# A decoder layer on one Trainium2 core: gates of two dense blocks written by accumulating scatters instead of one-hot products

## The chip, the cores and the metric

The kernel runs on one core of a Trainium2 chip. The metric is the time of one execution on the device in microseconds (us), as the median of several runs. The trace comes from a further execution, taken by the hardware profiler.

## What is computed

The program is one decoder layer for 512 tokens of width 1024: sparse attention and a state space mixer side by side, cross-attention to a memory, and an expert mixer. The change lies in the expert mixer (`peer_ffn`), which has 128 x 128 = 16384 experts of one neuron each. A token picks 16 experts in each of 8 heads, and its 128 gates go to softmax, head by head:

```python
s_top, i_top = lax.top_k(s, PEER_TOPK)                  # s: tokens x 8 heads x 2 sides x 128 keys
cand = (s_top[:, :, 0, :, None] + s_top[:, :, 1, None, :]).reshape(n, PEER_HEADS, PEER_TOPK * PEER_TOPK)
sc, ci = lax.top_k(cand, PEER_TOPK)
e_a = jnp.take_along_axis(i_top[:, :, 0], ci // PEER_TOPK, axis=-1)
e_b = jnp.take_along_axis(i_top[:, :, 1], ci % PEER_TOPK, axis=-1)
experts = e_a * PEER_N_KEYS + e_b
gw = jax.nn.softmax(sc, axis=-1)
act = jax.nn.gelu(jnp.einsum('td,tkd->tk', xb, u_tab[experts]))
out = jnp.einsum('tk,tkd->td', gw * act, v_tab[experts])
```

## The kernel before

The 512 tokens are four blocks of 128. Block 3 takes the experts' rows one by one: 256 gathers (128 rows of `utab`, `gather_u`, line 857; 128 of `vtab`, `gather_v`, line 870), each an indirect transfer of 128 rows of 4 KB that GpSimd issues, followed by a VectorE instruction over the landed tile (lines 859 and 874). The tiles `gr` come from a pool of seven buffers.

Blocks 0 to 2 (384 tokens) are dense: for each of the 128 values `a` of the first key, all 128 experts of that value are worked on for all 384 tokens. `layer1(a)` (line 840) loads 128 rows of u (512 KB), splits them in two parts (ScalarE makes `uh`, VectorE makes `ul`, lines 88 and 89), and multiplies them with the activations in 24 matmuls. `layer2(a)` (line 1072) multiplies that with a tile of gates (`mf`, line 1081), splits it and the rows of v, and `sum_up` adds 18 matmuls to the sums `yo` (line 1095). The gates are dense there too: a matrix of expert by token that is zero but for 128 values in each token's column. It lies in device memory as the tensor `wd`, and `load_w` (line 1098) brings in the gates of eight values of `a` at a time.

The stages in order of time:

- **Choosing** (lines 897 to 995). `project(h)` makes the scores of a head on TensorE; `head(h)` finds the best 16 on VectorE (lines 927 to 949); `decode(h)` turns positions into expert numbers (lines 952 to 983): `slA` and `slB` hold the two key numbers of each choice, `gidx` the expert number for block 3, `slW` the scores. `decode` of a head runs in the course of the next one. To keep TensorE busy, `keep_some` calls `layer1` for 76 values of `a` ahead of time and stores the results in device memory ("kept" products, `gd`); some gathers for block 3 are issued too (`P1G`).
- **Softmax** of all heads at once (lines 997 to 1004).
- **Gates** (lines 1034 to 1064). For each dense block, `turned` transposes `slA`, `slB` and `slW`; then, for each group of 16 tokens, VectorE builds four one-hot tiles (`oa`, `ob`, `obh`, `obl`, lines 1050 to 1053), TensorE multiplies them in 32 matmuls of 128 x 128 (`ps_w`, lines 1058 and 1059), ScalarE moves the result to `stg` in four instructions (line 1060), and a store of 1 MB writes it to `wd` (line 1062). Beside each of the 24 groups one or two more products are kept.
- **Summing** (lines 1134 to 1179): `layer2` and `sum_up` for all 128 values of `a`, `layer1` for the 52 that were not kept, and the rest of the gathers between them.

Within each engine instructions run in the order that a scheduler gave them when the program was built. SyncE issues the loads in such an order too; ScalarE issues the stores, GpSimd the gathers. Where one instruction needs another one's data, or its buffer, it waits for a semaphore, and all behind it on the same engine waits too.

Of the kernel before, what the change touches and what calls it, by code (L numbers as in the profile page):

```python
# [9 lines left out]
F32 = mybir.dt.float32  # L10
# [31 lines left out]
for _n, _w in (("ident", 128), ("tri", 128), ("cneg", 128), ("iota", 128),  # L42
               ("inv", 2)):
    CC[_n] = _at
    _at += _w
# [10 lines left out]
A8 = 8  # L56
P1G, P2G = 2, 0
NEARLY = 2
DELAY = 3
# [3 lines left out]
def tile_hybrid(ctx, tc, xT, memT, pos, prm, cst, win, wab, wsb, wou, wcq, wckv, wco, wpq, subk, uT, utab, vtab,  # L63
# [117 lines left out]
    atx = ExitStack()  # L181
    at = atx.enter_context(tc.tile_pool(name="at", bufs=1))
    wkA = ExitStack()
    wk = wkA.enter_context(tc.tile_pool(name="wk", bufs=2))
# [220 lines left out]
    def conv(j, dst):  # L405
# [15 lines left out]
        if j > 3:  # L421
            choose_some(3)

    zd = dram.tile([16, 128, T], F32, name="zd")
    gad = dram.tile([16, 128, T], F32, name="gad")

    def spill(ch, dst, func):
        ps = proj(ch)
        t = gen("spill")
        S.activation(t, ps, func, scale=0.5 if func == AF.Tanh else 1.0)  # L430
        S.dma_start(dst, t)

    for g in range(4):
        for j in range(4):
            conv(4 * g + j, xchunk(4 * g + j))
            spill(CH_Z + 4 * g + j, zd[4 * g + j], AF.Silu)
            if 4 * g + j:
                next(stepper, None)
        conv(16 + g, bT[g])
        conv(20 + g, cT[g])  # L440
# [342 lines left out]
    gp = ctx.enter_context(tc.tile_pool(name="gp", bufs=7, reuse_waits="tile"))  # L783
    wd = dram.tile([DENSE // TG, 128, 128 * TG], F32, name="wd")
    gd = dram.tile([N_KEPT, 128, DENSE], F32, name="gd")
# [134 lines left out]
    def head(h, sS, before):  # L920
# [22 lines left out]
        for b in order:  # L943
# [5 lines left out]
            V.max_index(ci[:, b, 8:16], slW[:, b, h * 16 + 8:h * 16 + 16], c_)  # L949
        return ci, ti  # L950

    def decode(h, ci, ti):

# [27 lines left out]
        for p, sl_ in ((0, slA), (1, slB)):  # L981
            V.tensor_tensor(sl_[:, :, hs], oh[:, 4 * p:4 * p + 4, 0], oh[:, 4 * p:4 * p + 4, 1], op=OP.add)
        V.scalar_tensor_tensor(gidx[:, hs], slA[:, 3, hs], 128.0, slB[:, 3, hs], op0=OP.mult, op1=OP.add)

    chosen = None
    sS = project(0)
    choosing[0] = True
    for h in range(9):
# [6 lines left out]
        chosen = nxt_chosen  # L995

    sw = slW.rearrange("p b (h s) -> p (b h) s", s=16)
    top = sp.tile([128, 32], F32, name="top", bufs=1)
    V.tensor_copy(top, sw[:, :, 0])
    V.tensor_tensor(sw, sw, top[:, :, None].to_broadcast([128, 32, 16]), op=OP.subtract)  # L1000
    S.activation(slW, slW, AF.Exp)
    V.tensor_reduce(top, sw, axis=AX.X, op=OP.add)
    V.reciprocal(top, top)
    V.tensor_tensor(sw, sw, top[:, :, None].to_broadcast([128, 32, 16]), op=OP.mult)
    V.tensor_copy(gwt, slW[:, 3, :])
# [27 lines left out]

    nxt = turned(0)
    for b in range(NTB):
        eT = nxt
        for g in range(128 // TG):
# [16 lines left out]
            for q in range(TG // 4):  # L1054
                ps = psum("sm", "ps_w")
                for i in range(4):
# [4 lines left out]
                             ps.rearrange("b (t a) -> b t a", t=4), AF.Copy, scale=1.0 / 32768)  # L1061
            S.dma_start(wd[b * (128 // TG) + g], stg.rearrange("b a t -> b (a t)"))
            keep_some(2 if b * 8 + g < NEARLY else 1)
            gather_some(P2G)
    keep_some(N_KEPT)
    se2.close()
# [31 lines left out]
    def load_w(j):  # L1098
        W8 = mp.tile([128, DENSE // TG, A8 * TG], F32, name="W8", tag="W8")
        SY.dma_start(W8, bass.AP(tensor=wd.tensor, offset=wd.offset + j * A8 * TG,  # L1100
                                 ap=[[128 * TG, 128], [128 * 128 * TG, DENSE // TG], [1, A8 * TG]]))
        return W8
# [79 lines left out]
def _constants():  # L1182
# [5 lines left out]
    for d, j in ((128, 0), (64, 1)):  # L1188
        half = d // 8
        inv = np.float32(500000.0) ** (np.float32(-2.0) * np.arange(half, dtype=np.float32) / np.float32(2 * half))  # L1190
        for base in range(0, 128, d):
            c[base:base + half, CC["inv"] + j] = inv
            c[base + 32:base + 32 + half, CC["inv"] + j] = -inv
    c[:, CC["iota"]:CC["iota"] + 128] = i[None, :]
    return c

# [76 lines left out]
```

## Time and profile before

| | |
|---|---|
| median of 3 runs | 2185.63 us (2183.03 to 2190.58) |
| the profiled execution | 2189.17 us, its span 2187.4 us |
| mean granted TensorE clock | 0.984 of full speed |
| busy in the span | TensorE 97%, VectorE 72%, ScalarE 45%, GpSimd 33% |
| moved by DMA | 469.26 MB, mean 215 GB/s |

The span runs from the first to the last instruction; the remaining 1.8 us of the execution lie around it. In the rows further down, PE is TensorE's matmuls, PEld its weight loads, DVE VectorE, ACT ScalarE, POOL GpSimd, and SPq the DMA queue of SyncE. A busy share is an average over stages with different limits, so the stages are read one by one.

### The profile page before, as it was taken

The page shows a single profiled execution, that of the slowest core. Times are in us where ns is not written, and L with a number is a line of the kernel's source. Part 1 is how long each engine was busy: PE and PEld are TensorE (multiplying, and loading weights), DVE is VectorE, ACT ScalarE, POOL GpSimd, SP SyncE. Part 2 cuts the span into 40 slices and gives each one's busy share as a digit, 9 for nine tenths or more (in the row PEclk, how much of TensorE's full clock was granted, in tenths as well). Part 3 has the DMA queues.
Part 4 walks back from the last instruction along what each step waited for, and adds up shares of the span by engine and source line. Part 5 has one row for each costly group of instructions (what it writes and reads, how often), then busy time and mean ns, then how long its engine had stood idle before and what let it go on. Part 6 is the DMA issues. An engine that isn't in the chain of part 4 may idle for free.

```text
span 2187.4 us, 29926 instructions
## 1 busy us (share of the span) xinstructions
PE 2111.0 (97%) x11039; PEld 1817.2 (83%) x11039; DVE 1575.6 (72%) x2954; ACT 977.2 (45%) x1513; POOL 718.7 (33%) x412
## 2 busy tenths in 40 slices
PE   8999999999999999999998999999999999999997
PEld 6888778877788777798988899988888888888886
DVE  8576744489952434499999588578778888788885
ACT  4444355665642334343434377643333333333333
POOL 2444432344324433204332000024344444444430
PEclk8999999999999999999999999999999999999999
DMA  4333322376453422248776477899999999999982
GB/s 136 110 109 115 105 90 85 106 213 179 144 177 98 130 78 82 101 138 315 262 244 223 133 259 260 287 324 367 333 327 336 339 352 327 341 330 327 345 287 70
DMA packets 209137, 469.26 MB, mean 215 GB/s; under 512 B 16064, under 2 KB 109376, under 8 KB 205792
## 3 DMA queue, kind: packets, MB, share of 16 engines
q1 hardware_dynamic: 153120, 284.63, 40.6%
q0 software_dynamic: 36864, 134.23, 16.7%
q10 hardware_dynamic: 19008, 48.51, 5.8%
q8 instruction: 86, 1.41, 0.3%
q14 instruction: 59, 0.48, 0.1%
HBM read 416.64 MB, written 50.66 MB: 214 GB/s over the span
## 4 chain that ended last, share of the span: by engine, by line
PE 78%; DVE 14%; ACT 3%; DMA 2%; issue 2%; POOL 1%; SPq 0%; DVEq 0%; ACTq 0%
PE yo L1095 24%; PE ps_u L138 18%; PE ps_in L138 15%; PE pss L138 4%; DVE ul L89 2%; PE ps_cq L138 2%; PE ps_h L138 2%; DVE gr L859 2%; PE ps_o L138 2%; PE ps_q L138 1%; PE ps_kv L138 1%; PE ps_w L1058 1%; PE ps_w L1059 1%; PE ps_l L459 1%; PE po L494 1%
## 5 line engine op out<-in xcount | busy, mean ns | idle before, releaser
L89 POOL TENSOR_TENSOR wl<-wr,wh 128x1024 fp32r<-128x1024 f32 x122 | 300.7, 2465 | 527.0 <-PE ps_in L138 166.7
L857 POOL DMA_INDIRECT gr<-utab,gidx x128 | 187.1, 1461 | 580.0 <-DVE gr L859 462.4
L138 PE MATMUL ps_u<-fH,uh 128*128 128x384 f32 x1024 | 349.5, 341 | 11.7 <-ACT uh L88 11.7
L138 PE MATMUL ps_u<-fL,uh 128*128 128x384 f32 x1024 | 345.7, 338 | 0.0
L870 POOL DMA_INDIRECT gr<-vtab,gidx x128 | 187.8, 1467 | 242.4 <-DVE acc L874 218.5
L88 ACT CAST vh<-vr 128x1024 fp32r<-128x1024 f32 x128 | 134.4, 1051 | 225.4 <-PE yo L1095 170.6
L138 PE MATMUL ps_in<-aH,wh 128*128 128x512 f32 x536 | 215.3, 402 | 4.0 <-ACT wh L88 2.8
L88 ACT CAST wh<-wr 128x1024 fp32r<-128x1024 f32 x135 | 141.3, 1047 | 167.9 <-PE ps_in L138 83.3
L138 PE MATMUL ps_in<-aL,wh 128*128 128x512 f32 x536 | 211.3, 395 | 0.3 <-DVE aL L89 0.3
L138 PE MATMUL ps_u<-fH,ul 128*128 128x384 f32 x1024 | 202.0, 338 | 9.7 <-DVE ul L89 9.3
L138 PEld LDWEIGHTS ps_u<-fH,uh 128*128 128x128 f32 x1024 | 194.2, 190 | 14.9 <-ACT uh L88 12.7
L1095 PE MATMUL yo<-vh,mh 128*128 128x512 f32 x768 | 199.0, 394 | 3.5 <-ACT mh L1085 3.5
L89 DVE TENSOR_TENSOR vl<-vr,vh 128x1024 fp32r<-128x1024 f32 x128 | 156.3, 1223 | 58.5 <-ACT vh L88 48.8
L1095 PE MATMUL yo<-vh,ml 128*128 128x512 f32 x768 | 198.4, 393 | 0.0
L1095 PE MATMUL yo<-vl,mh 128*128 128x512 f32 x768 | 197.5, 392 | 0.0
L138 PEld LDWEIGHTS ps_u<-fL,uh 128*128 128x128 f32 x1024 | 194.6, 190 | 1.9
L138 PEld LDWEIGHTS ps_u<-fH,ul 128*128 128x128 f32 x1024 | 180.6, 190 | 14.6 <-DVE ul L89 14.6
L89 DVE TENSOR_TENSOR ul<-ur,uh 128x1024 fp32r<-128x1024 f32 x82 | 103.6, 1265 | 120.5 <-ACT uh L88 65.0
L1095 PEld LDWEIGHTS yo<-vh,ml 128*128 128x128 f32 x768 | 145.1, 189 | 31.9
L1095 PEld LDWEIGHTS yo<-vl,mh 128*128 128x128 f32 x768 | 144.6, 188 | 31.7
L1095 PEld LDWEIGHTS yo<-vh,mh 128*128 128x128 f32 x768 | 144.2, 189 | 31.8 <-ACT mh L1085 3.8
L874 DVE SCALAR_TENSOR_TENSOR acc<-gr,gwt,acc 128x1024 f32<-128x1024 f32 x127 | 163.1, 1284 | 0.8
(450 smaller groups left out, 4032.2 us busy)
## 6 DMA issues: line engine op xcount, KB each, us to landing
vr<-vtab SPq DMA_DIRECT2D x128, 512.0 KB
ur<-uT SPq DMA_DIRECT2D x80, 512.0 KB
wr<-win SPq DMA_DIRECT2D x71, 512.0 KB
cr<-uT SPq DMA_DIRECT2D x48, 512.0 KB
wd<-stg ACTq DMA_DIRECT2D x24, 1024.0 KB
W<-wd SPq DMA_DIRECT2D x16, 1536.0 KB
gd<-ga ACTq DMA_DIRECT2D x76, 192.0 KB
gk<-gd SPq DMA_DIRECT2D x76, 192.0 KB
```

The source lines that it names most:

```text
L88: S.copy(hi, src)
L89: return (lo_eng or V).tensor_tensor(lo, src, hi.bitcast(F32), op=OP.subtract)
L138: TE.matmul(ps[:m, :n], w_[:, k, :m], x_[:, k, :n], start=first and i == 0, stop=last and i == len(order) - 1)
L459: TE.matmul(ps[:, :n], qT[:, b * 128:(b + 1) * 128], kT[h // 4][:, :n], start=True, stop=True)
L494: TE.matmul(po[:, b * 128:(b + 1) * 128], vt[:, s, (h // 4) * 128:(h // 4 + 1) * 128], pt[:, s * 128:(s + 1) * 128], start=s == 0, stop=s ...
L857: G.indirect_dma_start(out=r[:], out_offset=None, in_=utab[:, :], in_offset=bass.IndirectOffsetOnAxis(ap=gidx[:, k:k + 1], axis=0))
L859: return lambda: V.scalar_tensor_tensor(r, r, 1.0, afg, op0=OP.mult, op1=OP.mult, accum_out=gdot[:, k:k + 1])
L870: G.indirect_dma_start(out=r[:], out_offset=None, in_=vtab[:, :], in_offset=bass.IndirectOffsetOnAxis(ap=gidx[:, k:k + 1], axis=0))
L874: return lambda: V.scalar_tensor_tensor(acc, r, gwt[:, k:k + 1], acc, op0=OP.mult, op1=OP.add)
L1058: TE.matmul(w_ps, obh[at_], oa[at_], start=True, stop=False)
L1059: TE.matmul(w_ps, obl[at_], oa[at_], start=False, stop=True)
L1095: TE.matmul(yo[b][i], m[:, b * 128:(b + 1) * 128], v[:, i * 512:(i + 1) * 512], start=a == seq[0] and p == 0, stop=a == seq[-1] and p == 2)
```

## The change

The gates of blocks 0 and 1 are no longer made by one-hot products. `wd` becomes three tensors, one for each dense block. Those of blocks 0 and 1 are filled with zeros early in the program (`clear_gates`, 16 stores of 1 MB from SyncE). The softmax is done head by head: `head` makes the exponentials, `decode` the sums and the gates. `decode` then computes where each gate belongs (`wx`, from `slA`, `slB` and a new constant column `place`) and issues 16 indirect transfers for each of the two blocks. Each of them adds 128 single numbers, one for each token, to places in device memory. That is 32 in a head and 256 in all, 128 on each tensor. Block 2 keeps its eight groups of one-hot products. `P1G` goes from 2 to 0 (no gathers in the code of the heads); beside each group two products are kept, and the last twelve kept products have three gathers each beside them (`P3G`).

```diff
-P1G, P2G = 2, 0
-NEARLY = 2
+NSC = 2
+P1G, P3G = 0, 3
...
+    zeros = at.tile([128, 128], F32, name="zeros")
+    G.memset(zeros, 0.0)
...
+    wd = [dram.tile([128 * 128 * 128, 1], F32, name=f"wd{b}") for b in range(NTB)]
+    wdg = [w.rearrange("(g b f) o -> g b (f o)", b=128, f=128 * TG) for w in wd]
+
+    def clear_gates(i):
+        if i < NSC * (128 // TG):
+            w = wdg[i // (128 // TG)][i % (128 // TG)]
+            SY.dma_start(w.rearrange("b (r f) -> b r f", f=128), zeros[:, None, :].to_broadcast([128, TG, 128]))
...
             spill(CH_Z + 4 * g + j, zd[4 * g + j], AF.Silu)
+            clear_gates(4 * g + j)
...
-        return ci, ti
-
-    def decode(h, ci, ti):
+        ex = sp.tile([128, 4, 16], F32, name="ex", tag="ex")
+        hw = slW[:, :, h * 16:(h + 1) * 16]
+        V.tensor_tensor(ex, hw, hw[:, :, 0:1].to_broadcast([128, 4, 16]), op=OP.subtract)
+        S.activation(ex, ex, AF.Exp)
+        return ci, ti, ex
+
+    def decode(h, ci, ti, ex):
...
+        sm = sp.tile([128, 4], F32, name="sm", tag="sm")
+        V.tensor_reduce(sm, ex, axis=AX.X, op=OP.add)
+        V.reciprocal(sm, sm)
+        V.tensor_tensor(slW[:, :, hs], ex, sm[:, :, None].to_broadcast([128, 4, 16]), op=OP.mult)
+        wi = sp.tile([128, NSC, 16], F32, name="wi", tag="wi")
+        V.tensor_scalar(wi, slA[:, :NSC, hs], float(TG), cs[:, CC["place"]:CC["place"] + 1], op0=OP.mult, op1=OP.add)
+        wx = sq.tile([128, NSC, 16], I32, name="wx", tag="wx")
+        V.scalar_tensor_tensor(wx, slB[:, :NSC, hs], float(128 * TG), wi, op0=OP.mult, op1=OP.add)
+        for s in range(16):
+            for b in range(NSC):
+                G.indirect_dma_start(out=wd[b][:, :], out_offset=bass.IndirectOffsetOnAxis(ap=wx[:, b, s:s + 1], axis=0),
+                                     in_=slW[:, b, h * 16 + s:h * 16 + s + 1], in_offset=None, compute_op=OP.add)
...
-    nxt = turned(0)
-    for b in range(NTB):
+    nxt = turned(NSC)
+    for b in range(NSC, NTB):
...
-            S.dma_start(wd[b * (128 // TG) + g], stg.rearrange("b a t -> b (a t)"))
-            keep_some(2 if b * 8 + g < NEARLY else 1)
-            gather_some(P2G)
-    keep_some(N_KEPT)
+            S.dma_start(wdg[b][g], stg.rearrange("b a t -> b (a t)"))
+            keep_some(2)
+    while kept[0] < N_KEPT:
+        keep_some(1)
+        gather_some(P3G)
...
-        SY.dma_start(W8, bass.AP(tensor=wd.tensor, offset=wd.offset + j * A8 * TG,
-                                 ap=[[128 * TG, 128], [128 * 128 * TG, DENSE // TG], [1, A8 * TG]]))
+        for b in range(NTB):
+            SY.dma_start(W8[:, b * (128 // TG):(b + 1) * (128 // TG), :],
+                         wdg[b][:, :, j * A8 * TG:(j + 1) * A8 * TG].rearrange("g b f -> b g f"))
```

The scheduler orders the changed program anew. Three places matter. In these rows a number behind a name tells buffers apart, and the brackets name the semaphores that a row waits for: `DMASW` with a number counts the ends of GpSimd's transfers, which take the numbers 0 to 7 in turn; `DMAHW` those of other transfers; the rest are engines. The first is GpSimd's queue from the first expert numbers on. Before:

```order
L89 TENSOR_TENSOR fL<-ft,fH 128x512 x4
L857 DMA gr<-utab,gidx 128x1024 x128
L870 DMA gr<-vtab,gidx 128x1024 x128
L1123 TENSOR_TENSOR htm<-htm,gf 128x1024 x2
L1269 UNCONDITIONAL_BRANCH
```

In the change (`wd0` and `wd1` are the gates of blocks 0 and 1):

```order
L89 TENSOR_TENSOR fL_7320<-ft_7424,fH_7319 128x512 [waits Activation_49]
L868 DMA gr_11795<-utab,gidx_7324 128x1024 [waits DVE_49]
L1009 DMA wd0_493<-slW_7342,wx_8031 2097152x1 [waits DVE_49]
L1009 DMA wd1_494<-slW_7342,wx_8031 2097152x1
L868 DMA gr_11797<-utab,gidx_7324 128x1024 [waits Pool_49]
L1009 DMA wd0_493<-slW_7342,wx_8031 2097152x1 [waits DMASW1_49]
L1009 DMA wd1_494<-slW_7342,wx_8031 2097152x1 [waits DMASW2_49]
L868 DMA gr_11799<-utab,gidx_7324 128x1024 [waits Pool_49]
L1009 DMA wd0_493<-slW_7342,wx_8031 2097152x1 [waits DMASW4_49]
L1009 DMA wd1_494<-slW_7342,wx_8031 2097152x1 [waits DMASW5_49,DMASW0_49]
L868 DMA gr_11835<-utab,gidx_7324 128x1024
```

The 256 scatters stand where gathers stood, in pairs, one for each tensor. With the numbers counted on from 0 at the first gather, the first scatter on `wd0` has 1, and the next one on `wd0` waits for 1: each scatter waits for the end of the one before it on the same tensor. 34 gathers stand between pairs, all of them ahead of the scatters of head 3; the other 222 stand behind the last scatter. The second place is VectorE, where the positions `wx` of head 2 are made. Before, `gidx` follows its two inputs with no wait for a transfer:

```order
L930 MAX tv_8988<-sS_8543 128x8 [waits DVE_49]
L982 TENSOR_TENSOR slA_7320<-oh_8719 128x4x16 [waits DVE_49]
L982 TENSOR_TENSOR slB_7321<-oh_8719 128x4x16
L931 MAX_INDEX ti_8989<-tv_8988,sS_8543 128x8 [waits DVE_49]
L983 SCALAR_TENSOR_TENSOR gidx_7303<-slA_7320,slB_7321 128x16 [waits DVE_49]
L928 MAX_INDEX ti_8989<-tv_8988,sS_8543 128x8
```

In the change:

```order
L997 TENSOR_TENSOR slA_7340<-oh_8786 128x4x16 [waits DVE_49]
L997 TENSOR_TENSOR slB_7341<-oh_8786 128x4x16
L1004 TENSOR_SCALAR wi_8799<-slA_7340,cs_60 128x32 [waits DVE_49]
L998 SCALAR_TENSOR_TENSOR gidx_7324<-slA_7340,slB_7341 128x16 [waits DVE_49]
L942 MAX_INDEX ti_9075<-tv_9074,sS_8610 128x8
L1006 SCALAR_TENSOR_TENSOR wx_8801<-slB_7341,wi_8799 128x32 [waits DMASW4_49,DMASW3_49,DMASW6_49,DMASW1_49,DMASW7_49,DMASW0_49,DVE_49]
L939 MAX_INDEX ti_9075<-tv_9074,sS_8610 128x8 x2
L89 TENSOR_TENSOR ul_8892<-cr_8889,uh_8891 128x1024 [waits DMAHW2_49,PE_49,Activation_49]
```

`wx` has two buffers, so that of head h waits for the scatters of head h - 2, and the split `ul` of a kept product stands behind it. In this order 26 of the 76 kept products have their `ul` behind the `wx` of head 7. The third place is SyncE's queue around the first load of gates, `W8`. Before, all loads of u for kept products stand ahead of it, and one for a fresh product (`ur_12801`):

```order
L827 DMA ur_12754<-uT 128x1024 [waits DMAHW7_49,DMAHW1_49,DVE_49]
L1075 DMA vr_12838<-vtab 128x1024 [waits DMAHW0_49,PE_49]
L1075 DMA vr_12903<-vtab 128x1024 [waits DMAHW2_49]
L1075 DMA vr_12939<-vtab 128x1024 [waits DMAHW3_49]
L827 DMA ur_12801<-uT 128x1024 [waits DMAHW5_49,DMAHW4_49,DVE_49]
L1110 DMA gf_12799<-gfin 128x1024 [waits DMAHW7_49,PE_49]
L1100 DMA W8_12834<-wd_7312 128x24x128 [waits DMAHW4_49,DMAHW6_49,DMAHW1_49,PE_49]
```

In the change:

```order
L838 DMA ur_11841<-uT 128x1024 [waits DMAHW7_49,DMAHW1_49,DVE_49]
L1120 DMA W8_12314<-wd0_493 128x8x128 [waits DMASW4_49,DMASW5_49,DMASW3_49,DMASW6_49,DMASW2_49,DMASW7_49,DMASW1_49,DMAHW5_49,DMASW0_49,PE_49]
L838 DMA ur_11881<-uT 128x1024 [waits DMAHW3_49,DMAHW2_49,DVE_49]
L1120 DMA W8_12314<-wd1_494 128x8x128
L838 DMA ur_11924<-uT 128x1024 [waits DMAHW7_49,DMAHW5_49,DVE_49]
L1120 DMA W8_12314<-wd2_495 128x8x128 [waits DMAHW6_49,DMAHW4_49,DMAHW0_49]
```

The load of gates waits for the last scatters of both tensors, and the loads of u for the last nine kept products and for three further ones stand behind it. All twelve products stand ahead of the first `yo` matmul on TensorE; before, there was one fresh product there, so two of them are work of the summing stage done earlier.

## Rows read from the trace of the kernel before

**Rows 1.** The page: busy us, share and instructions of each engine.

```profile
PE 2111.0 (97%) x11039; PEld 1817.2 (83%) x11039; DVE 1575.6 (72%) x2954; ACT 977.2 (45%) x1513; POOL 718.7 (33%) x412
```

**Rows 2.** Stretches of the span: busy us of each engine, TensorE clock, DMA.

```profile
core 0: us, PE busy (x) PEld busy (x) DVE busy (x) ACT busy (x) POOL busy (x), PEclk, DMA share, GB/s
0.00:928.00 928.00, 894.99 (x4430) 721.12 (x4431) 547.81 (x915) 433.88 (x816) 339.11 (x154) 0.98 0.39 121
928.00:1240.00 312.00, 298.31 (x1613) 279.36 (x1612) 279.63 (x1112) 126.89 (x162) 73.73 (x55) 0.99 0.66 222
1240.00:1420.00 180.00, 168.25 (x1443) 164.07 (x1444) 144.98 (x136) 128.60 (x149) 0.00 (x0) 0.96 0.71 256
1420.00:2187.00 767.00, 749.47 (x3557) 652.63 (x3555) 603.22 (x792) 287.83 (x387) 305.89 (x203) 0.99 0.90 314
```

**Rows 3.** The matmuls and the evictions of the one-hot products, ns min/median/max.

```profile
L1058 PE MATMUL ps_w<-oa,obh x384: 218/218/312, 1244.2 to 1408.0; 128*128 128x128 f16 x192
...
L1060 ACT ACTIVATE stg<-ps_w x96: 1052/1124/1168, 1246.3 to 1409.6; 128x512 f32<-128x512 f32 x96
```

**Rows 4.** TensorE in time, one-hot products: start, length, [idle before <-releaser].

```profile
1244.16 0.61 PE L1058 MATMUL ps_w<-oa,obh 128*128 128x128 f16 x4 [5.40 <-DVE obh L1052]
...
1256.37 0.24 PE L1058 MATMUL ps_w<-oa,obh 128*128 128x128 f16 x1
...
1258.19 0.42 PE L138 MATMUL ps_u<-fH,uh 128*128 128x384 f32 x1
```

**Rows 5.** Groups of instructions, a one-hot tile: busy us, mean ns.

```profile
L1050 DVE TENSOR_TENSOR oa<-io,e 128x2048 f16<-128x2048 f16 x24 | 29.3, 1219 | 0.0
```

**Rows 6.** TensorE in time, kept products one after another.

```profile
1412.35 0.33 PE L138 MATMUL ps_u<-fH,uh 128*128 128x384 f32 x1
...
1416.51 0.33 PE L138 MATMUL ps_u<-fH,uh 128*128 128x384 f32 x1
...
1419.28 1.55 PE L138 MATMUL ps_u<-fH,ul 128*128 128x384 f32 x8
```

**Rows 7.** The expert numbers of eight heads, first and last start.

```profile
L983 DVE SCALAR_TENSOR_TENSOR gidx<-slA,slB x8: 146/154/174, 982.7 to 1204.7; 128x16 int32<-128x16 f32 x8
```

**Rows 8.** GpSimd in time, gathers back to back and one after a wait.

```profile
983.16 1.11 POOL L857 DMA_INDIRECT gr<-utab,gidx  x1 [61.43 <-DVE ti L928]
...
990.19 0.94 POOL L857 DMA_INDIRECT gr<-utab,gidx  x1 [0.30 <-issue]
991.43 0.94 POOL L857 DMA_INDIRECT gr<-utab,gidx  x1 [0.30 <-issue]
992.68 0.94 POOL L857 DMA_INDIRECT gr<-utab,gidx  x1 [0.30 <-issue]
...
1010.25 1.68 POOL L857 DMA_INDIRECT gr<-utab,gidx  x1 [2.35 <-DVE gr L859]
```

**Rows 9.** VectorE in time, the first gathers landing.

```profile
987.85 1.23 DVE L859 SCALAR_TENSOR_TENSOR gr<-gr,afg 128x1024 f32<-128x1024 f32 x1 [0.63 <-DMA gr<-utab,gidx]
...
996.97 1.23 DVE L859 SCALAR_TENSOR_TENSOR gr<-gr,afg 128x1024 f32<-128x1024 f32 x1 [0.48 <-DMA gr<-utab,gidx]
...
1002.91 1.22 DVE L859 SCALAR_TENSOR_TENSOR gr<-gr,afg 128x1024 f32<-128x1024 f32 x1 [0.45 <-DMA gr<-utab,gidx]
```

**Rows 10.** The start in time: a small load, its user, a table load.

```profile
0.75 1.28 ACT L337 ACT_TABLE_LOAD   x1 [0.75 <-PEq L1262]
0.75 0.38 SPq L194 DMA_DIRECT2D pr<-prm  x1
...
2.71 0.20 ACT L337 ACTIVATE na<-pr 32x1 f32<-32x1 f32 x1 [0.68 <-DMA pr<-prm]
```

**Rows 11.** The first load of gates and its user in time.

```profile
1420.22 0.38 SPq L1100 DMA_DIRECT2D W<-wd  x1
...
1429.00 0.56 DVE L1081 TENSOR_TENSOR mf<-gk,W 128x384 f32<-128x384 f32 x1 [2.18 <-DMA gk<-gd]
```

**Rows 12.** TensorE in time, the first matmuls of the sums.

```profile
1430.15 2.07 PE L1095 MATMUL yo<-vh,mh 128*128 128x512 f32 x4 [3.51 <-ACT mh L1085]
```

More of the change, by code (lines that the diff above doesn't have):

```diff
@@ L42 @@
 for _n, _w in (("ident", 128), ("tri", 128), ("cneg", 128), ("iota", 128),
-               ("inv", 2)):
+               ("inv", 2), ("place", 1)):
     CC[_n] = _at
@@ L783, in tile_hybrid @@
     gp = ctx.enter_context(tc.tile_pool(name="gp", bufs=7, reuse_waits="tile"))
-    wd = dram.tile([DENSE // TG, 128, 128 * TG], F32, name="wd")
     gd = dram.tile([N_KEPT, 128, DENSE], F32, name="gd")
@@ L995, in tile_hybrid @@
         chosen = nxt_chosen
[L997 to L1004, printed above, removed]
     V.tensor_copy(gwt, slW[:, 3, :])
@@ L1194, in _constants @@
     c[:, CC["iota"]:CC["iota"] + 128] = i[None, :]
+    c[:, CC["place"]] = i // TG * (128 * 128 * TG) + i % TG
     return c
```

## The prediction, written before the changed kernel ran

> **What bounds the kernel now.** The page's busy times come first: TensorE is busy for 2111 of 2187.4 us [rows 1], so work taken off TensorE shortens the kernel as long as nothing else makes it wait. The table by stretches shows where the change acts [rows 2]. Ahead of 928 us nothing of it runs but the zero fill. From 928 to 1240 (choosing) TensorE is busy for 298 of 312 us and VectorE for 280, so both are nearly full. From 1240 to 1420 (gates and kept products) TensorE is busy for 168 of 180 us and GpSimd does nothing. From 1420 on (summing) TensorE is busy for 749 of 767 us at a DMA share of 0.90. So a microsecond of TensorE in the gates' stage is worth about one, while GpSimd has time to spare on average. What decides is whether GpSimd's new work ends in time, since the sums can't begin without the gates.
>
> **What is taken away.** A group of one-hot products lasts 1.82 us on TensorE once it runs, from 1256.37 to 1258.19 [rows 4]; 16 of the 24 groups go: 16 x 1.82 = 29 us off TensorE's path. The wait of 5.40 us ahead of the first group [rows 4] stays, since block 2 has a first group too. VectorE loses four tiles of 1.22 us in each group [rows 5], 16 x 4 x 1.22 = 78 us, and ScalarE four evictions of 1.12 us [rows 3], 72 us. Neither bounds that stage, so these count nothing. The most that can be won is about 30 us.
>
> **Small additions, counted as nothing.** The zero fill is 16 MB in a stretch whose DMA share is 0.39 and where TensorE is busy for 895 of 928 us [rows 2]; at the 314 GB/s of the summing stage it is 53 us of transfers in 16 portions. Behind a portion a weight load is some 3 us late, which the loads' lead should cover; without that cover it would be up to 53 us. The exponentials by head bring two table loads to each head, 1.28 us each [rows 10], 16 x 1.28 = 20 us on ScalarE, which is busy for 127 of 312 us while heads are chosen. Fourteen more gathers are left for the summing stage (222 against 208), 7 MB or 23 us at its rate, and 18 us of VectorE; a tenth of 767 us of DMA time is free there, so TensorE covers them, and bare they would cost 23 us.
>
> **What is added to a path: the chain of scatters.** Each scatter waits for the end of the one before it on the same tensor, and the two tensors go side by side. So 128 pairs follow each other, and the length of a pair is the larger of two things: GpSimd's time to issue two scatters (three transfers where a gather stands between), or the time from a scatter's start on GpSimd to its last write.
>
> *Issue.* The trace has no scatter; the nearest row is a gather, which also makes 128 rows of descriptors from a list. Back to back they start every 1.24 us (990.19, 991.43, 992.68) [rows 8]. Two make 2.48 us, three 3.72 us. After a real wait one takes 1.68 us where 0.94 is usual [rows 8].
>
> *End of a scatter, from below.* A small plain load, issued at 0.75 us, has its user start at 2.71: 1.96 us [rows 10]. An indirect transfer has GpSimd's part besides; but if an end came within 2.48 us, issue would bound the pair.
>
> *From above.* The first gather starts at 983.16 on GpSimd [rows 8] and its user, which waited for it, at 987.85 [rows 9]: 4.69 us, with 512 KB moved. A scatter moves 512 bytes but reads its places before it writes them, so even this isn't a firm ceiling.
>
> *What I take.* The nearest row is the gather without its payload. The fourth to the seventh gather land in 996.97 to 1002.91 [rows 9], 1.98 us each, so the payload is some 2.0 us and 2.7 us are left. That gather took 1.11 us on GpSimd; after a wait, as every scatter, it is 1.68, which adds 0.6. For the reading before the writing I add another 0.6, an estimate between nothing and a second trip of 1.96 us. So a pair takes 3.9 us, with a gather between 3.9 + 1.24 = 5.1 us. 34 pairs have a gather, 94 have none: 34 x 5.1 + 94 x 3.9 = 173 + 367 = 540 us.
>
> **From the chain to the end.** The chain begins with the first expert numbers, written at 982.7 [rows 7]; I take 984 for the added softmax. It ends at 984 + 540 = 1524 us. The heads can't run ahead of it: `wx` has two buffers, so VectorE stands before each new `wx` until the scatters two heads back are done. A head needs 31.7 us now (seven steps from 982.7 to 1204.7 [rows 7]), against 16 x 3.9 = 62 us for its scatters. TensorE's kept products run dry as their `ul` stands behind `wx` on VectorE. At the end SyncE's load of gates waits for the last scatter, and behind it stand the loads of u for nine kept and three fresh products, ahead of the first `yo` on TensorE. From the last scatter: about 8 us for the gates and the first u (the load of gates now takes from 1420.22 to 1429.00 until it is used [rows 11]), then 12 x 4.16 us (a kept product, 1412.35 to 1416.51 [rows 6]) = 50 us. So the first `yo` comes at 1524 + 58 = 1582, against 1430.15 now [rows 12]. Two of the fresh products are summing work done early, 8 us. The summing stage itself keeps its length. The sum is 1582 - 1430 - 8 = 144 us later: the profiled execution, 2189.2 us now, would take 2333. The median of the runs shown lies 3.5 us below it, so I forecast **2330 us**, slower by 6.6%. In general the shift is 34 x (p + 1.24) + 94 x p - 396 for a pair of p us, and nothing is won or lost at p = 2.8 us.
>
> **Rival 1: issue bounds the pairs, and the kernel is faster.** If a scatter ends within 2.48 us of its start, the chain takes 34 x 3.72 + 94 x 2.48 = 360 us and ends at 1344. Then TensorE's work behind the last `wx` decides. That `wx` waits for the scatters of head 5, 984 + 34 x 3.72 + 62 x 2.48 = 1264; behind it are 26 kept products (108 us), eight groups (15 us), the 5.4 us and some 2 us of start, so the kept products end near 1394, against 1420.8 now (1419.28 + 1.55 [rows 6]). That is 26 us sooner: **2160 us**. For it: 1.96 us is seen for a small load. Against it: the gather without its payload is above 2.48 already, and GpSimd's part after a wait is longer. It decides below p = 2.8. The Trainium skill speaks for this rival: its page "DMA: Bandwidth & Descriptors", section "Anatomy of one DMA — SWDGE (gpsimd) path", fits a transfer issued by GpSimd as 2.0 us and its bytes over 436 GB/s, so a scatter would end in 2.0 us and this rival's time would follow. By that fit the first gather would have landed in 3.2 us, and the row has 4.69 [rows 9], so the trace doesn't agree, and I leave this rival the smaller chance. The same page (section "Rules for kernel authors") says that an accumulating transfer must wait for the semaphore of an earlier one on the same bytes; the order of the change has that wait, and no run yet shows its price.
>
> **Rival 2: adding in memory is dear.** If the read, add and write of the eight numbers that each of the 16 DMA engines has follow each other with no overlap, a scatter costs 1.7 us and several trips of 1.96 us [rows 10]. With only two in a row behind one another it is 5.6 us: 34 x 6.8 + 94 x 5.6 - 396 = +362 us, **2548 us**; with eight it would be far more. Nothing in the trace speaks for or against it.
>
> **Rival 3: the parts cancel.** Near p = 2.8 the chain eats the 29 us: 2180 to 2192 us.
>
> **Chances.** About 0.3% (6.6 us) is what a measurement of this kernel can tell from no change. The forecast's own mechanism, a pair bound by the scatter's end, has 0.65; its own range goes from p = 3.28 (nothing for reading before writing: +66 us, 2252) to p = 4.69 (a gather's whole time: +247 us, 2433). Rival 1 has 0.22, rival 2 has 0.08, rival 3 has 0.05. So faster 0.22, same 0.05, slower 0.73. The range has to reach rival 1 and leaves out rival 2 and what the forecast has above p = 4.7: 2157 to 2435 us.
>
> **What would show it.** In the changed profile, scatters on GpSimd in pairs about 3.9 us apart in the heads without gathers, each after a wait for the transfer before it on its tensor; the last one near 1524 us; VectorE idle before `wx` and before `mf`, waiting for `wd`; TensorE busy well below 80% from 1000 to 1530 us; the summing stage some 750 us as now. I am wrong if pairs come every 2.5 us (rival 1), or above 5 us (rival 2), if TensorE stays full while the chain runs, or if time goes to the stretch ahead of 928 us (the zero fill) or into the summing stage (the gathers left over).

## The result, and the profile after

The changed kernel takes **2396.4 us** (2393.8 to 2398.7, 4 runs) against 2185.3 us (2183.0 to 2190.6) for the kernel before on the same chip: a ratio of 1.0961, 95% interval 1.0945 to 1.0978. It is slower by 211 us; 2330 us was forecast. The profiled execution of the change takes 2395.6 us (span 2393.8), 206 us above the 2189.2 us of the profiled execution before.

The page's busy times after the change:

```profile
PE 2088.0 (87%) x10521; PEld 1797.0 (75%) x10521; DVE 1507.7 (63%) x2923; ACT 931.8 (39%) x1468; POOL 1149.3 (48%) x669
```

The products of the sums on TensorE (ns min/median/max, first and last start):

```profile
L1114 PE MATMUL yo<-vh,mh x768: 387/392/397, 1639.3 to 2379.4; 128*128 128x512 f32 x192
```

TensorE lost 23 us of work against [rows 1], and its share fell from 97% to 87%. The first `yo` comes at 1639.3 us instead of 1430.2 [rows 12]: 209 us later, which with sums 3 us shorter is the whole loss. The stretches answer to [rows 2], cut at the new start of the sums (busy us of each engine, then TensorE's clock, DMA share, GB/s):

```profile
0.00:928.00 928.00, 891.74 (x4445) 718.60 (x4446) 550.29 (x920) 435.96 (x819) 339.04 (x155) 0.99 0.45 139
928.00:1240.00 312.00, 214.40 (x1076) 197.63 (x1075) 198.14 (x877) 94.92 (x122) 210.32 (x134) 0.85 0.57 145
1240.00:1420.00 180.00, 97.56 (x523) 93.99 (x522) 64.70 (x235) 44.98 (x57) 139.18 (x84) 0.77 0.43 78
1420.00:1639.00 219.00, 142.59 (x951) 140.55 (x952) 79.55 (x72) 75.20 (x92) 132.58 (x77) 0.81 0.63 171
1639.00:2393.00 754.00, 741.73 (x3531) 646.25 (x3530) 615.00 (x821) 280.76 (x380) 328.16 (x221) 0.99 0.90 323
```

Ahead of 928 us and in the sums (754 us, 757 before) nothing is lost. Between them TensorE stands for a third of the time, while GpSimd, idle from 1240 to 1420 before, is busy for 139 of 180 us. The scatters, and who waits for whom around them (us, times):

```profile
L1009 POOL DMA_INDIRECT wd<-slW,wx x256: 1557/1564/2732, 981.9 to 1582.0; - x128
...
its engine sat idle before it (us, times) until:
  issue: 63.3, 206
  DMA wd<-slW,wx: 53.0, 49
...
who waited for it (us, times):
  DVE wx L1006: 154.3, 4
  POOL wd L1009: 53.0, 49
```

A second wait of VectorE (us in total, times, longest):

```profile
DVE gr L870 <- DMA gr<-utab,gidx: 63.2, 16, 14.8
```

The chain runs from 981.9 to 1583.5 us, 601.6 us, and consists almost wholly of GpSimd itself: 433 us of scatters (256 of 1.69 us on average), 42 us of 33 gathers between them (the 34th stands ahead of the first scatter), 73 us of steps of 0.30 us from one instruction to the next, and only **53 us** of waits for an earlier scatter, of which 15 us would have been steps anyway. That is not the picture of the prediction, in which the waits set the pace. VectorE stands before `wx` for 154 us, as forecast, and for another 63 us at tiles whose gathers stand between scatters on GpSimd; before, that second wait was 5 us in the choosing stage. GpSimd in time, a quiet piece and one beside VectorE's work:

```profile
1424.18 1.56 POOL L1009 DMA_INDIRECT wd<-slW,wx  x1 [0.30 <-issue]
1426.05 1.56 POOL L1009 DMA_INDIRECT wd<-slW,wx  x1 [0.30 <-issue]
1427.91 1.56 POOL L1009 DMA_INDIRECT wd<-slW,wx  x1 [0.30 <-issue]
...
1453.83 2.50 POOL L1009 DMA_INDIRECT wd<-slW,wx  x1 [0.91 <-DMA wd<-slW,wx]
1456.63 2.55 POOL L1009 DMA_INDIRECT wd<-slW,wx  x1 [0.30 <-issue]
1459.48 2.58 POOL L1009 DMA_INDIRECT wd<-slW,wx  x1 [0.30 <-issue]
```

In the quiet piece a scatter follows the last every 1.87 us with no wait for a transfer, a pair every 3.73. In the other one the records themselves are 2.5 us long. VectorE at those places:

```profile
1438.43 0.19 DVE L1006 SCALAR_TENSOR_TENSOR wx<-slB,wi 128x32 int32<-128x32 f32 x1 [37.71 <-DMA wd<-slW,wx]
...
1456.52 1.23 DVE L89 TENSOR_TENSOR ul<-ur,uh 128x1024 fp32r<-128x1024 f32 x1 [1.63 <-ACT uh L88]
1458.27 1.22 DVE L1070 TENSOR_TENSOR obh<-ob,whh 128x2048 f16<-128x2048 f16 x1 [0.52 <-PE ps_w L1076]
1459.41 1.22 DVE L1068 TENSOR_TENSOR oa<-io,e 128x2048 f16<-128x2048 f16 x1
```

It stood ahead of `wx` for 37.71 us, through the quiet piece; as soon as it works, the scatters get longer. Sorted by what ran beside them, the 121 scatters with no VectorE instruction all lie below 1.60 us (mean 1.56); of the 49 that lay mostly beside the subtraction for `ul` (L89) 24 are above 1.65, mean 1.88; all six beside `obl` (L1071) are, mean 2.26.

Pairs with no gather between take 3.73 us at least, 3.77 in the median and 4.33 on average (94 of them); with a gather 5.79 on average (33). From the last scatter to the first `yo` TensorE runs 240 matmuls, which at 24 a product are ten products:

```profile
1583.50:1639.30 55.80, 45.53 (x240) 45.21 (x241) 21.18 (x22) 19.39 (x26) 5.70 (x4) 0.86 0.91 309
```

### The profile page after: what moved, and what is told of

Its sections match the earlier page's. It is cut to its first block, busy times and chain, and to the rows that moved or that the text cites. A ratio compares the mean times of both kernels' runs of the same rounds, so it can differ in the third digit from the quotient of the medians.

```text
span 2393.8 us, 29121 instructions
## 1 busy us (share of the span) xinstructions
PE 2088.0 (87%) x10521; PEld 1797.0 (75%) x10521; DVE 1507.7 (63%) x2923; ACT 931.8 (39%) x1468; POOL 1149.3 (48%) x669
## 4 chain that ended last, share of the span: by engine, by line
PE 63%; POOL 11%; DMA 10%; DVE 8%; issue 5%; ACT 2%; SPq 0%; DVEq 0%; ACTq 0%; POOLq 0%
PE yo L1114 22%; PE ps_in L138 14%; PE ps_u L138 11%; POOL wd L1009 10%; DMA wd<-slW,wx 8%; PE pss L138 4%; PE ps_cq L138 2%; PE ps_h L138 2%; PE ps_o L138 2%; PE ps_q L138 1%; PE ps_kv L138 1%; PE ps_l L471 1%; POOL gr L868 1%; PE po L506 1%; DVE ul L89 1%
## 5 line engine op out<-in xcount | busy, mean ns | idle before, releaser
L89 POOL TENSOR_TENSOR wl<-wr,wh 128x1024 fp32r<-128x1024 f32 x122 | 300.0, 2460 | 525.9 <-PE ps_in L138 166.1
L1009 POOL DMA_INDIRECT wd<-slW,wx x256 | 433.3, 1693 | 116.6 <-issue 63.3
L138 PE MATMUL ps_u<-fH,ul 128*128 128x384 f32 x1024 | 209.9, 348 | 154.0 <-DVE ul L89 154.0
L138 PEld LDWEIGHTS ps_u<-fH,ul 128*128 128x128 f32 x1024 | 186.8, 196 | 158.7 <-DVE ul L89 158.7
L138 PEld LDWEIGHTS ps_u<-fH,uh 128*128 128x128 f32 x1024 | 199.1, 194 | 57.4 <-ACT uh L88 55.1
L89 DVE TENSOR_TENSOR ul<-ur,uh 128x1024 fp32r<-128x1024 f32 x82 | 103.8, 1266 | 179.3 <-ACT uh L88 139.4
L89 DVE TENSOR_TENSOR vl<-vr,vh 128x1024 fp32r<-128x1024 f32 x128 | 156.5, 1223 | 63.8 <-ACT vh L88 55.4
L870 DVE SCALAR_TENSOR_TENSOR gr<-gr,afg 128x1024 f32<-128x1024 f32 x128 | 152.7, 1222 | 63.2 <-DMA gr<-utab,gidx 63.2
L88 ACT CAST uh<-ur 128x1024 fp32r<-128x1024 f32 x82 | 86.2, 1051 | 225.5 <-PE ps_u L138 142.5
```

The source lines that it names most:

```text
L88: S.copy(hi, src)
L89: return (lo_eng or V).tensor_tensor(lo, src, hi.bitcast(F32), op=OP.subtract)
L138: TE.matmul(ps[:m, :n], w_[:, k, :m], x_[:, k, :n], start=first and i == 0, stop=last and i == len(order) - 1)
L870: return lambda: V.scalar_tensor_tensor(r, r, 1.0, afg, op0=OP.mult, op1=OP.mult, accum_out=gdot[:, k:k + 1])
L1009: G.indirect_dma_start(out=wd[b][:, :], out_offset=bass.IndirectOffsetOnAxis(ap=wx[:, b, s:s + 1], axis=0), in_=slW[:, b, h * 16 + s:h * 1 ...
```

## The experiments

**Theory I** (issue): GpSimd's own time for a scatter sets the pair. **Theory E** (end, the prediction's): the time to a scatter's last write sets it. The runs, each timed beside the kernel before on the same chip; "chain" is from the first scatter's start to the last one's end on GpSimd. Runs 1, 2, 3, 6 and 8 leave out some of the gates or of their adding, as each says, so they show what a part costs and are no kernels to use:

| run | median us | ratio to before, 95% | chain us | first `yo` |
|---|---|---|---|---|
| the change | 2396.4 | 1.0961 (1.0945 to 1.0978) | 601.6 | 1639.3 |
| 1 four tensors | 2369.2 | 1.0841 (1.0823 to 1.0859) | 574.0 | 1611.3 |
| 2 no adding | 2296.8 | 1.0500 (1.0483 to 1.0518) | 505.9 | 1547.6 |
| 3 half the slots | 2195.6 | 1.0042 (1.0025 to 1.0059) | 346.5 | 1438.7 |
| 4 eight `wx` | 2388.0 | 1.0918 (1.0900 to 1.0936) | 595.5 | 1636.7 |
| 5 late gates | 2362.4 | 1.0807 (1.0782 to 1.0832) | 605.1 | 1603.7 |
| 6 half, late gates | 2157.0 | 0.9863 (0.9839 to 0.9887) | 366.8 | 1401.1 |
| 7 one block | 2334.4 | 1.0669 (1.0639 to 1.0698) | 574.5 | 1590.4 |
| 8 one block, two tensors | 2211.1 | 1.0116 (1.0093 to 1.0140) | 393.4 | 1462.6 |
| 9 no gathers between | 2416.8 | 1.1049 (1.1025 to 1.1073) | 530.4 | 1661.6 |
| 10 one block, complete | 2236.1 | 1.0231 (1.0212 to 1.0249) | 291.5 | 1471.3 |
| 11 the same, gathers late | 2190.4 | 1.0016 (1.0006 to 1.0026) | 324.4 | 1413.1 |
| 12 no gathers until sums | 2347.6 | 1.0736 (1.0720 to 1.0752) | 569.2 | 1578.5 |

### 1. Four tensors: take the waits away

```diff
+    wq = [wd, [dram.tile([128 * 128 * 128, 1], F32, name=f"wo{b}") for b in range(NTB)]]
...
-                G.indirect_dma_start(out=wd[b][:, :], ...
+                G.indirect_dma_start(out=wq[s % 2][b][:, :], ...
```

> What differs from the changed kernel: the scatters of odd slots go to two more tensors, so each scatter waits for the one four places back and not two. The gates of odd slots are not added to the others (nothing reads the two new tensors). Theory I (issue): the changed kernel's pairs are bound by GpSimd's own time, 1.56 us for a scatter and 0.30 us between two, and waits for transfers are only 53 us of the chain of 601 us. Then the records stay at 1.56 us, the waits go, the chain is 530 to 560 us (256 x 1.87 + 33 gathers x 1.57 = 530), and the kernel takes 2325 to 2355 us. Theory E (end, the one of the prediction): the pair lasts as long as a scatter takes to its last write, and the issue of a scatter is 1.24 us as that of a gather, so that 1.56 us is a record stretched by transfers in flight. Then the records shrink, and the chain falls towards 128 x 2.48 + 34 x 1.24 = 360 us: 2160 to 2200 us.

The scatters of the two sets, and the time from issue to landing (us min/median/max):

```profile
L1010 POOL DMA_INDIRECT wd<-slW,wx x128: 1552/1558/2708, 981.2 to 1549.5; - x128
L1010 POOL DMA_INDIRECT wo<-slW,wx x128: 1557/1557/2610, 986.1 to 1553.7; - x128
...
  DMA wd<-slW,wx: 0.3, 1
...
  DMA wo<-slW,wx: 0.3, 1
...
DMA to landing us min/median/max: 2.9/3.4/8.5
```

The waits are gone (0.6 us), the records stay at 1.56 us in the median, and the chain loses only 28 of the 53 us. Theory E's 360 us did not come; theory I is right in kind, but chain (574 us) and time (2369 us) lie above its ranges: 15 of the 53 us were steps anyway, and the scatters became longer (mean 1.75 us).

### 2. No adding

```diff
-                                     ..., in_offset=None, compute_op=OP.add)
+                                     ..., in_offset=None)
```

> What differs from the changed kernel: the scatters write their numbers and do not add them, so where two heads of a token chose the same expert the later gate stands alone. The waits stay as they are. Theory I (issue, the time is that of making 128 descriptors for single numbers): a scatter still takes 1.56 us on GpSimd, the chain loses at most the 53 us of waits, 2345 to 2400 us. Theory A (adding is the price, on GpSimd or in the transfer): the record falls to the 1.0 us of a gather and the chain to some 128 x 2.6 + 33 x 1.3 = 376 us, 2170 to 2200 us; if only the transfer's end is earlier, the waits alone go, 2340 us.

```profile
L1009 POOL DMA_INDIRECT wd<-slW,wx x256: 963/970/2098, 985.7 to 1490.6; - x128
...
  DMA wd<-slW,wx: 107.5, 77
...
DMA to landing us min/median/max: 2.1/2.8/6.5
```

A scatter that only writes takes 0.97 us on GpSimd, nearly as a gather does (0.94): **adding costs 0.59 us of GpSimd for each scatter**, which theory I had put at nothing. Landing, which the trace gives for about half of the transfers, is 0.6 us earlier over the whole chain (2.8 against 3.4 in run 1). But these medians mix quiet pieces with others. In a piece in which VectorE stands and no gather is near, run 1 (from 1300 to 1352 us) and run 2 (from 1237 to 1258 us) have:

```profile
DMA to landing us min/median/max: 2.9/3.1/3.1
...
DMA to landing us min/median/max: 2.1/2.1/3.8
```

There adding costs 0.9 us from start to landing: the 0.59 us on GpSimd and some 0.3 us behind it (1.5 against 1.2 us from the end of the record to landing). With the issue of a pair down to 2.54 us the waits double to 107.5 us, and the chain keeps 506 us: now the ends bound many of the pairs. The time, 2297 us, lies between the ranges of both theories. No run took adding and waits away together.

### 3 and 6. Half the slots: what the rest of the change is worth

```diff
-        for s in range(16):
+        for s in range(0, 16, 2):
```

> What differs from the changed kernel: only the eight even slots of each head are scattered, 128 transfers in place of 256; the gates of the odd slots are left out. Both theories see the chain fall to 64 pairs of 4.4 us and 33 gathers, 64 x 4.4 + 33 x 1.24 = 322 us, so that it ends near 1304 us, when TensorE still has kept products to do. Then the first product of the summing stage comes near 1404 us, where TensorE's own work ends (1430 less the 29 us of one-hot products and some start), and the kernel takes 2155 to 2185 us. A third view (something else that the change adds, such as the softmax by head, the zero fill or the gathers left over, costs some tens of us) would leave it at 2200 us or above.

The chain takes 346 us where 322 were expected, VectorE still stands before `wx` for 40 us, and the kernel is 0.4% slower than the one before. Whether something else in the change ate the rest was settled by run 6, with the edits of runs 4 and 5 added:

> What differs from the kernel with half the slots (eight even slots of each head are scattered, the gates of the odd slots are left out): eight wx and the late load of gates. With half the slots alone the chain of 346 us made VectorE stand before wx for 40 us and the result was 0.4% above the kernel before. If the chain, through these two waits, is the whole loss, then this kernel shows what the rest of the change is worth: 16 groups of one-hot products off TensorE, 29 us, less a few us, 2155 to 2170 us. If something else in the change costs time (softmax by head, zero fill, gathers left over), it stays at 2175 us or above.

2157 us, 29.7 us under the kernel before, with the first `yo` 29 us sooner: the 16 groups were worth 29 us, as the prediction had it. The zero fill, the softmax by head and the gathers left over cost nothing together that shows. So the loss lies in the chain and in what waits for it.

### 4 and 5. The two places that wait for the chain

```diff
-        wx = sq.tile([128, NSC, 16], I32, name="wx", tag="wx")
+        wx = sp.tile([128, NSC, 16], I32, name="wx", tag="wx", bufs=8)
```

> What differs from the changed kernel: wx has eight buffers, in the pool of the choosing stage, so VectorE no longer stands before a wx until the scatters two heads back are done. Theory I and theory E agree that the chain on GpSimd stays some 600 us and ends near 1584 us; the kept products are then all done by then, and the nine of them that came behind the last scatter are saved: 9 x 4.16 = 37 us, 2350 to 2365 us. If instead VectorE's stall were what held the chain up (a head's scatters late because its wx was late), the chain would shorten and the time fall below 2300 us. If the busier DMA engines slow the scatters' ends, the chain gets longer and the gain is under 20 us.

Only 8 us, and that expectation was wrong by the prediction's own step: SyncE's queue holds the loads of u for the last nine kept products behind the load of gates, and eight `wx` don't change that. TensorE now works through to 1392 us and then stands past the last scatter, to 1589; the first `yo` still comes 55.8 us behind it. Two stretches of that run:

```profile
1240.00:1384.00 144.00, 137.09 (x948) 135.42 (x948) 80.11 (x86) 76.08 (x93) 105.53 (x59) 0.98 0.73 192
1388.00:1580.00 192.00, 4.24 (x25) 3.92 (x23) 0.00 (x0) 0.00 (x0) 160.59 (x104) 0.52 0.23 0
```

While VectorE works (the first), a scatter takes 2.48 us from start to start, with 27 waits of 29 us in all; while all others stand (the second), 1.87 us, without one wait in 103 scatters. Run 5 moved the load, with the eight `wx` kept:

```diff
+            with tc.issue_after(last_load[0].ins):
-            SY.dma_start(W8[...], ...)
+                SY.dma_start(W8[...], ...)
```

> What differs from the kernel with eight wx: SyncE's first load of gates stands behind the load of u for the last kept product, where nine of these loads stood behind it. Theory I: the chain keeps its 600 us, so it ends near 1583 us. All kept products are done by then, and of the 56 us from the last scatter to the first product of the summing stage only the gates' load and the fresh products are left, 10 to 25 us: 2350 to 2362 us. If instead the kernel stays at 2388 us, it was not the place of these loads on SyncE that cost the 56 us.

The first `yo` now comes 17 us behind the last scatter instead of 56. The chain was 10 us longer this time, and the time stands at the upper end of the range.

### 7 and 8. One block: the end of a scatter by itself

```diff
-NSC = 2
-P1G, P3G = 0, 3
+NSC = 1
+P1G, P3G = 2, 0
```

> What differs from the kernel before: only block 0 gets its gates by scatters, 128 of them, all on one tensor, with eight wx and the late load of gates, and two gathers beside each step of a head as in the kernel before. Each scatter must wait for the one right before it, so the chain shows the time from a scatter's start to its last write, whatever the issue. Theory I: no end was seen below 2.55 us and pairs with no wait took 3.7 to 4.6 us, so an end takes 3 to 3.5 us in quiet and some 4.4 us beside other work: 128 x 3.0 to 4.4 = 384 to 563 us with the gathers inside, ending between 1366 and 1545 us; the kernel takes between 2170 us (the chain ends while TensorE still works, eight groups or 15 us are won) and 2310 us. Theory E in its own numbers (an end takes 3.9 us): 128 x 3.9 = 499 us, ending at 1483 us, 2240 us.

Each scatter now waits for the one just before it (GpSimd while all other engines stand):

```profile
1546.68 1.55 POOL L1009 DMA_INDIRECT wd<-slW,wx  x1 [1.68 <-DMA wd<-slW,wx]
1549.91 1.55 POOL L1009 DMA_INDIRECT wd<-slW,wx  x1 [1.68 <-DMA wd<-slW,wx]
1553.18 1.55 POOL L1009 DMA_INDIRECT wd<-slW,wx  x1 [1.72 <-DMA wd<-slW,wx]
```

From start to start 3.3 us in quiet (18 scatters from 1500 us on), and over the 117 that waited 3.89 us in the median, 4.44 on average, 11.6 at most. So the prediction's 3.9 us for an end was right in the median, and theory I's 4.4 beside other work on average. The chain (574 us) and the time (2334 us) lie above all that was expected. The time is not clean: VectorE waited 123 us for a scatter before it could write a tile of the sums (`vl`), it seems because `wx` lies in the memory that the tile uses next. Run 8 took a second tensor:

> What differs from the kernel with one block: odd slots go to a second tensor, so that a scatter waits for the one two places back. The gates of odd slots are not added to the others (nothing reads the second tensor). Theory I: 128 scatters of 1.87 us and some 48 gathers of 1.57 us, stretched by VectorE and some waits to 2.2 us a scatter, make 128 x 2.2 + 48 x 1.57 = 357 us, the chain ends near 1340 us, while TensorE still has kept products, and eight groups of one-hot products are won: 2168 to 2180 us. If the chain is longer than 440 us it ends behind TensorE's work, and the kernel is slower than before.

393 us and 2211 us, a miss. The chain did end before TensorE's work, but in the choosing stage TensorE was busy for 236 of 300 us (1000 to 1300) where it was 283 before: GpSimd's gathers stand behind scatters, and VectorE stood 60 us for gathered tiles.

### 9 and 12. Both blocks with no gathers between

```diff
-        G.indirect_dma_start(out=r[:], out_offset=None, in_=utab[:, :], ...
+        with tc.issue_after(last_sc[0].ins):
+            G.indirect_dma_start(out=r[:], out_offset=None, in_=utab[:, :], ...
```

> What differs from the kernel with eight wx and the late load of gates: no gather is issued before the last scatter (33 stood between the pairs). The formula of the prediction with the measured pair, p = 4.33 us without and p + 1.24 with a gather, gives 128 x 4.33 = 554 us for the chain in place of 605, so it ends near 1536 us and the kernel takes 2362 - 51 = 2311 us (2300 to 2325). If pairs with a gather are only bound by the transfer's end (the gather then hides in a wait), taking the gathers out gains nothing: 2350 us or more. The floor by GpSimd's own time alone is 256 x 1.87 = 479 us: 2236 us, still slower than before.

The chain fell by 75 us to 530, more than the formula's 51, and yet the kernel got slower, 2417 us. VectorE's longest wait:

```profile
DVE gr L873 <- DMA gr<-utab,gidx: 292.1, 2, 291.8
```

An instruction on a gathered tile stood in VectorE's order ahead of the one-hot tiles, and its gather now stood behind all scatters on GpSimd. Run 12 leaves all gathers to the sums (`P3G` is 0 there):

> What differs from the changed kernel: eight wx, the late load of gates, and no gathers at all before the summing stage, so nothing on VectorE waits behind the scatters. The chain of both blocks is then that of the run before it, 530 us, from 981 to 1512 us, and the first product of the summing stage comes 17 us behind its end (as with the late load of gates: 1586.5 to 1603.7), at 1529 us. The summing stage has all 256 gathers and some 760 us. So 2190.2 + 1529 - 1430 + 5 = 2294 us (2285 to 2305): slower than before even with every wait around the chain taken away. If the time falls below 2240 us, the chain was held up by something that these edits removed.

2348 us, 54 us above what was expected; the profiled execution is 58 us above it. Of these, 39 are the chain, 569 us instead of 530: in run 9 VectorE had stood for 292 us, and here the scatters' records are 12 us longer in all and the waits between them 27 us. Another 11 us are its later start and a longer way to the first `yo` (24.5 us instead of 17), and some 9 are the sums, 772 us long with 34 more gathers. Even so the step is clear: of the four kernels that kept all 256 adding scatters and changed only buffers and order (runs 4, 5, 9 and 12) none came nearer than 7.4%.

### 10 and 11. A complete version with half the scatters

One block by scatters on two tensors, both cleared, both loaded and added by VectorE; then gathers late:

```diff
+                W9 = mp.tile([128, 128 // TG, A8 * TG], F32, name="W9", tag="W9", bufs=1)
+                SY.dma_start(W9, wog[b][:, :, j * A8 * TG:(j + 1) * A8 * TG].rearrange("g b f -> b g f"))
...
+                V.tensor_tensor(W0, W0, W9, op=OP.add)
```

> What differs from the kernel with one block on two tensors: nothing is left out (the second tensor is cleared too, loaded beside the first one and added by VectorE, 16 x 1.22 = 20 us), and no gather is issued before the last scatter; gathers stand beside the one-hot groups instead. Theory I: 128 scatters of 1.87 to 2.2 us, 240 to 282 us, run inside the choosing of the heads (254 us), so the chain ends near 1270 us and holds nothing up; 8 groups or 15 us come off TensorE, and what stands against it is 8 MB more of loads (25 us at 323 GB/s in a stage whose DMA share is 0.90) and VectorE's 20 us in the summing stage: 2165 to 2185 us, 0 to 1% faster than before. If scatters still stretch the choosing stage as with gathers between them, 2190 to 2215 us.

2236 us, above both ranges. The chain (292 us) is out of the way, but VectorE stood 68 us at a gathered tile. With that removed:

> What differs from the complete kernel with one block: gathers stand only beside the last nine groups of one-hot products, and VectorE's instruction on a gathered tile is placed behind the group that it belongs to; before, VectorE stood for 72 us at such a tile while GpSimd still worked on the scatters, and TensorE ran dry with it. Theory I: the 76 us that TensorE waited for are saved, with some 4 us back for gathers left to the summing stage (229 in place of 208): 2158 to 2175 us, faster than the kernel before by 0.5 to 1.3%. If the summing stage, whose DMA share is 0.94 to 1.00 with the second tensor's loads, is bound by its transfers, 2180 to 2200 us.

```profile
928.00:1240.00 312.00, 306.60 (x1742) 292.40 (x1741) 255.73 (x1078) 152.52 (x193) 184.56 (x104) 0.99 0.56 139
1240.00:1413.00 173.00, 155.00 (x1165) 151.55 (x1163) 120.89 (x128) 100.35 (x120) 81.69 (x50) 0.97 0.95 321
1413.00:2195.00 782.00, 746.33 (x3456) 643.26 (x3456) 637.29 (x857) 260.54 (x376) 360.61 (x233) 0.97 0.93 330
```

The sums begin 17 us sooner than in [rows 12] and last 782 us where they lasted 757: what half the scatters win, the longer sums give back, and the kernel is level with the one before (0.16% above). Run 10, with the same second tensor but 210 gathers in its sums instead of 231, has sums of 762 us, so gathers left over weigh there: the two runs lie 21 us apart. No complete version beat it.

## Why the prediction was right, and where it was off

- **The sign and the place** were right: nothing lost ahead of 928 us or in the sums; TensorE starved from 1000 to 1639 us by VectorE's waits for `wx` (154 us) and by SyncE's order. VectorE's 63 us at gathered tiles are a third wait, which the prediction did not have.
- **The 29 us won and the small additions at nothing**: run 6, 29.7 us.
- **From the last scatter to the first `yo`**: 58 us forecast, 55.8 measured; run 5 shows that 39 of them are SyncE's order. That the two lie so close is in part luck: the sum has twelve products, and TensorE ran ten there (nine kept and one fresh), in 47.7 us and not 41.6, with a wait of 2.1 us between and at a granted clock of 0.86. The section on the change is wrong there too: twelve loads of u stand behind the load of gates, but only ten products ahead of the first `yo`.
- **The size was off by 62 us** in the profiled execution (206 against 144). The mis-sized term is the length of a pair, "So a pair takes 3.9 us": it measured 4.33 on average and 5.79 with a gather (forecast 5.1). The chain took 601.6 us instead of 540; with that chain the prediction's formula gives 601.6 - 396 = 206 us, which is what was lost. Of the 62 us, 57 are the later first `yo` (1639 against 1582 us). The other 5 are the two products of the summing stage that were to be done early, for 8 us: as many fresh products run behind the first `yo` as before (51), so none was, and the sums are only 3 us shorter.
- **The step that failed inside it** is the issue, "Two make 2.48 us", read from gathers. An adding scatter takes 1.56 us on GpSimd where a gather takes 0.94, so two make 3.73 us. That alone lies above the break-even of 2.8 us. The end that the prediction took for the bound (3.3 us in quiet, 3.89 in the median, run 7) is about as long, so the two limits lie side by side: without waits a pair still takes 4.09 us (run 1, 103 pairs without a gather), without adding 3.64 (run 2).
- **A row was misread.** That a gather "after a real wait" takes 1.68 us [rows 8] was put down to the wait. In the trace before, 63 of the 94 gathers that lay mostly beside VectorE's subtractions of L89 took over 1.65 us, and none of the 20 with no VectorE instruction beside them took over 0.95; the scatters of the change show the same.
- **That 3.9 us was near the end's median is luck in its parts.** Without adding an end takes 2.1 us in quiet (run 2) where 2.7 were taken, the 0.6 us for the wait are not the wait's, and adding costs 0.9 us there where 0.6 were taken. In quiet that makes 3.0 us, 3.3 with the step to the next scatter; the rest of the 3.89 us goes with other work beside the scatters, for which the prediction's sum has no term of its own.
- **Rival 1** (issue bounds, faster) had half the truth: issue is a bound, but at 3.73 us. It rested on an issue that no scatter with adding has. The fit that the Trainium skill gives for GpSimd's transfers ("DMA: Bandwidth & Descriptors", section "Anatomy of one DMA — SWDGE (gpsimd) path"), 2.0 us for so few bytes, is nearly met in quiet by a scatter that does not add (2.1 us, run 2). Over the whole chain it is not: 2.8 us in the median without adding, 3.4 with it (runs 2 and 1). **Rival 2** (adding dear in memory) was wrong in its place and size: of the 0.9 us that adding costs in quiet 0.59 are on GpSimd.

## What to carry to other kernels

Before replacing matrix work by many small transfers, count the issuing engine's own time for each of them, in the very form that is to be used, beside the engine that it will run next to; waits between transfers come on top of that. A chain that others wait for is paid three times: in itself, in whatever stands behind its waiters on their queues (loads of u behind a load of gates, one-hot tiles behind a gathered tile), and in what the freed engines then do to it. What such a chain is worth without its cost can be measured by halving it (run 6).

## What was not expected of the hardware

- Adding made GpSimd's part of an indirect transfer of 128 single numbers longer, from 0.97 to 1.56 us, and the time behind it only from 1.2 to 1.5 us in quiet (runs 2 and 1).
- Beside VectorE's instructions on two tiles these records are longer, 2.26 us on average beside L1071. A chain on GpSimd was quicker while VectorE stood (run 9 against run 12: 530 and 569 us), though only 12 of these 39 us are in the records and 27 in waits for ends. The Trainium skill ("SBUF — State Buffer", section "Who interferes with whom") says that such an instruction contends with GpSimd's reads and that in a probe it did not hold up transfers; the records here show GpSimd held up while it issues them. Which access it is held up at, no run here shows.
- In the stretch of run 4 in which TensorE stands the granted clock is 0.52, near the lower level of 1.2 GHz, and 0.98 in the one before it, in which TensorE is busy.
